# Two-layer encoder on one core: first transfers, step rates, and layer 0's attention and short convolution

## Chip, cores and metric

One core of a Trainium2 chip runs the whole kernel in one launch. The metric is the device time of a launch in microseconds (us). PE is TensorE (the matrix engine), DVE is VectorE, ACT is ScalarE, POOL is GpSimd, and SP is SyncE, whose queue issues all DMA transfers of this kernel.

## The reference

The input is x (256 positions, 2048 channels), a condition c (2048 values) and fp32 weights for two layers; everything is computed and returned in fp32. Cut to what matters:

```
c_act = silu(c)
for l in range(2):
    shift_m, scale_m, gate_m, shift_f, scale_f, gate_f = (c_act @ w_mod[l] + b_mod[l]) in 6 parts
    h = layer_norm(x) * (1 + scale_m) + shift_m
    uv, q_c, kv_c, k_r, sb, sc, sh, ag = split(h @ w_in[l])       # 4288 columns
    y_a = gelu(u) * spatial gating of layer_norm(gelu(v))
    y_b = latent attention: q = rms_norm(q_c) @ w_uq, k and v = rms_norm(kv_c) @ w_ukv,
          rotary parts on q and on k_r, softmax over a block-causal mask, 4 heads
    y_c = sb * conv3(sc * sh)                                     # short causal convolution
    y_d = silu(layer_norm(conv31(a * sigmoid(g))))                # a, g from ag
    x = layer_norm(ALPHA * x + (1 + gate_m) * (concat(y_a, y_b, y_c, y_d) @ w_out[l]))
    h = layer_norm(x) * (1 + scale_f) + shift_f
    x = layer_norm(ALPHA * x + (1 + gate_f) * ((silu(conv3(gate)) * val) @ w_down[l]))   # gate, val = h @ w_up[l]
```

## The kernel before

The 2048 channels are 16 tiles of 128 (KT = 16), the positions two tiles of 128. Weights stream from memory in units of 1 MB or less and are used once.

**Two ways to multiply.** A plain ("exact") unit loads fp32 weights into a buffer named `wexact` and PE multiplies them as fp32; the trace has two matmul instructions for each such product. A split unit loads into `wraw` (one of four raw buffers of 1 MB, shared with `wmod`), ACT rounds it to a high half `whi` (L390), DVE subtracts to get the low half `wlo` (L391), and PE does three products in place of one exact product: high by high, low by high, high by low. The activations are split the same way by ACT and DVE (`a`, L409 and L410). Layer 0's input projection and the last two column chunks of its output projection are exact, as are the first `PLAIN_UNITS` units of the first chunk; nearly all the rest is split.

**Modulation steps.** `w_mod` is read in 192 blocks of 1 MB. A block is one DVE instruction over 128x2048: a product with the condition's rows `crep` summed into a column (L194), or, for a gate, an accumulation of rows into `macc` (L205). Layer 0's first 32 blocks feed its first norm. The other 160 are doled out by a generator, `mods`: each unit that is loaded calls `pump`, which adds the phase's rate from `RATES` to a credit and takes one step for each whole credit. `need` takes what is missing at the place where a result is wanted. `STEPS` says how many background steps (the taps of the 31-wide convolution, L870 on ACT and L873 on DVE) run with a unit.

**Order.** Each engine runs its instructions in one fixed order. The tile framework makes that order when the kernel is built: by the program's order, with instructions that its own timing holds for ready let ahead. A `NoSync` dependency fixes the order of two instructions on one engine.

**Start.** The transfers are issued as: identity (`cst`), parameters (`par`), condition row (`crow`), the two halves of x, then `w_mod` and `w_in` blocks in turn. PE spreads `crow` over 128 rows (`ps_c`), ACT makes `crep` of it. DVE takes the statistics of x (L1466), POOL the power, and then DVE the first two `wmod` blocks, which wait for the power. ACT scales x (`xn`), PE transposes it (L1489), ACT modulates it (`hF`, L118), and the first products `D_c` run. After the transposes of the two halves, `warm` puts 8 and 14 products of the identity with itself on PE (`spare`, L1475; two instructions each).

**Layer 0's attention.** When the latents' sums are there (`B_w`, `B_n`), `mix_b` takes `MODS_AHEAD` gate steps, then ACT copies the latents to `lat`. In `attend`, PE turns them through two PSUM buffers that alternate (`ps_q`, `ps_q`, `ps_kv`, `ps_kr`, `ps_qn` and so on): ACT scales the queries' part `qg`, DVE forms the key's products `kc` (L1079, L1080) and the latents `kvr` (L1084), both kept behind the steps taken ahead, and PE then forms `ps_kr` and the queries `ps_qn`. The softmax takes maximum, reciprocal, scaling (L1177) and the copies of the turned probabilities (L1191 to L1195) on DVE, the exponential on ACT. The rest of layer 0's input projection (`C_c`) runs between these pieces. The short convolution `conv_c` has one ACT scaling and two DVE accumulations for each of 4 channel tiles (L1250, L1252).

**Output projection.** `out_proj` goes through three column chunks (1024, 512 and 512 wide); in the first, a unit is two channel tiles, 8 units in all. DVE adds the gate and the residual (`yg`, L632 on), and the norm follows.

Of the kernel before, what the change touches and what calls it, by code (L numbers as in the profile page):

```python
# [13 lines left out]
P = 128  # L14
# [18 lines left out]


RATES = [
    dict(B=1.3, attend=1.3, C=1.9, out=1.0, out_next=1.55, out_last=0.0, up=0.7, down=0.7, down_next=0.7, down_last=0.0),
    dict(D=1.0, U=0.0, V=0.0, B=0.0, C=0.0, E=0.9, attend=0.0, out=0.6, out_next=0.6, out_last=0.0, up=0.3, down=0.7, down_next=0.7, down_last=0.0),
]

STEPS = [  # L40
# [46 lines left out]
def encoder_kernel(ctx: ExitStack, tc: tile.TileContext, A: dict, consts: bass.AP, out: bass.AP):  # L87
    nc = tc.nc
    pe, act, dve, pool = nc.tensor, nc.scalar, nc.vector, nc.gpsimd

    keep = ctx.enter_context(tc.tile_pool(name="keep", bufs=1))
    rawp = ctx.enter_context(tc.tile_pool(name="rawp", bufs=4))
    splitp = ctx.enter_context(tc.tile_pool(name="splitp", bufs=4))
# [50 lines left out]
    def power(o, i):  # L144
        return pool.tensor_tensor(out=o, in0=i, in1=mhalf[:, : i.shape[1]], op=ALU.pow)

    X = []
    for t in range(2):
        x_t = keep.tile([P, D], F32, name=f"x{t}")
        X.append(x_t)  # L150

    par = keep.tile([P, -(-PARAMS // 16) * 16], F32, name="par")
    nc.sync.dma_start(out=par[:, 0:112], in_=A["params"][:, 0:112])
    crow = raw_tile("crow")
    nc.sync.dma_start(out=crow[0:1, :], in_=A["c"])
    for t in range(2):
        nc.sync.dma_start(out=X[t], in_=A["x"][0, t * P : (t + 1) * P, :])
    cact = keep.tile([P, 16], F32, name="cact")
    act.activation(out=cact, in_=par[:, 0:16], func=AF.Silu)

    crep = keep.tile([P, D], F32, name="crep")
    for i in range(4):
# [12 lines left out]
    plus_one(0, SCALE_M)  # L175
# [6 lines left out]


    MOD = {}
    last_step = [None]
    data_dep = mybir.DependencyInfo(mybir.DependencyClass.Sync, mybir.DependencyReason.DATA)
    order_dep = mybir.DependencyInfo(mybir.DependencyClass.NoSync, mybir.DependencyReason.DATA)

    def mod_block(l, m, kt, col):

# [9 lines left out]
    def mod_step(acc, w, kt, first):  # L200
        col = cact[:, kt : kt + 1]
        if first:
            i = dve.tensor_scalar(out=acc, in0=w, scalar1=col, scalar2=None, op0=ALU.mult)
        else:
            i = dve.scalar_tensor_tensor(out=acc, in0=w, scalar=col, in1=acc, op0=ALU.mult, op1=ALU.add)  # L205
        held(i, "mod")
        last_step[0] = i.ins.name

    def gate_rows(l, m, acc):

# [579 lines left out]
    def mixers(l, w_in, Y, hF=None, first_mod=None, quarter=None):  # L790
# [265 lines left out]
        def attend(WQ, WKV, lat, q01, rr):  # L1056
# [20 lines left out]
            by = turn(ps, S, [lat[t][:, 256:320] for t in range(2)])  # L1077
            kc = tmp_tile("kc")
            behind(dve.tensor_tensor(out=kc[0:64, 0:S], in0=by[0:64, :], in1=cosT[0:64, :], op=ALU.mult))  # L1079
            dve.tensor_tensor(out=kc[0:64, S : 2 * S], in0=by[0:64, :], in1=sinT[0:64, :], op=ALU.mult)  # L1080
            ps = ms_tile("ps_kv")
            for j in range(2):
                by = turn(ps, j * S, [lat[t][:, j * P : (j + 1) * P] for t in range(2)])
                behind(dve.tensor_scalar(out=kvr[:, j, :], in0=by, scalar1=KVG(j), scalar2=None, op0=ALU.mult))  # L1084

            rope = slot("rope").rearrange("p (j s) -> p j s", j=4)
            ps = ms_tile("ps_kr")
# [55 lines left out]
            def softmax(blk, g):  # L1143
                nkey = P * (blk + 1)
                per = 512 // nkey
                ps = ms_tile("ps_sc")
                for i in range(per):
                    h = g * per + i
                    o = ps[:, i * nkey : (i + 1) * nkey]
                    qs = slice(blk * P, (blk + 1) * P)  # L1150
                    mm(o, qn[:, h, qs], kn[:, h, :nkey], True, False)
                    mm(o, rope[:, h // 2, qs], rope[:, 2 + h % 2, :nkey], False, True)
                sm = smallp.tile([P, 16], F32, tag="sm", name="sm", bufs=3)
                p3 = ps.rearrange("p (i k) -> p i k", i=per)
                dve.memset(p3[0:64, :, nkey - 64 :], NEG)
                dve.tensor_reduce(out=sm[:, 0:per], in_=p3, axis=AX.X, op=ALU.max)
                dve.tensor_scalar(
                    out=sm[:, 4 : 4 + per],
                    in0=sm[:, 0:per],
                    scalar1=rr[:, 4 + blk : 5 + blk],  # L1160
                    scalar2=-1.0,
                    op0=ALU.mult,
                    op1=ALU.mult,
                )
                pt = tmp_tile("p")
                for i in range(per):
                    act.activation(
                        out=pt[:, i * nkey : (i + 1) * nkey],
                        in_=ps[:, i * nkey : (i + 1) * nkey],
                        func=AF.Exp,  # L1170
                        scale=rr[:, 4 + blk : 5 + blk],
                        bias=sm[:, 4 + i : 5 + i],
                        accum_out=sm[:, 8 + i : 9 + i],
                    )
                dve.reciprocal(out=sm[:, 12 : 12 + per], in_=sm[:, 8 : 8 + per])
                for i in range(per):
                    dve.tensor_scalar(  # L1177
                        out=pt[:, i * nkey : (i + 1) * nkey],
                        in0=pt[:, i * nkey : (i + 1) * nkey],
                        scalar1=sm[:, 12 + i : 13 + i],  # L1180
                        scalar2=None,
                        op0=ALU.mult,
                    )
                return pt

            def turned(pt, blk, g):
                ps = ms_tile("ps_pT")
                for i in range(4):
                    pe.transpose(ps[:, i * P : (i + 1) * P], pt[:, i * P : (i + 1) * P], ident)
                if blk == 0:  # L1190
                    dve.tensor_copy(pT0[:, :, 0:P], ps.rearrange("p (h s) -> p h s", h=4))  # L1191
                else:
                    p4 = ps.rearrange("p (h k s) -> p h k s", h=2, k=2)
                    dve.tensor_copy(pT0[:, 2 * g : 2 * g + 2, P : 2 * P], p4[:, :, 0, :])
                    dve.tensor_copy(pT1[:, 2 * g : 2 * g + 2, :], p4[:, :, 1, :])  # L1195

            p0 = softmax(0, 0)
            p1 = softmax(1, 0)
# [47 lines left out]

        def conv_c(ch):
            yc = Y["c"] = slot("yc").rearrange("p (j s) -> p j s", j=4)
            for j in range(4):
                act.activation(out=yc[:, j, :], in_=ch[:, j, :], func=AF.Copy, scale=SW(2, j))  # L1250
                for k in range(2):
                    dve.scalar_tensor_tensor(  # L1252
                        out=yc[:, j, 2 - k :],
                        in0=ch[:, j, : S - 2 + k],
                        scalar=SW(k, j),
                        in1=yc[:, j, 2 - k :],
                        op0=ALU.mult,
                        op1=ALU.add,
                    )
# [200 lines left out]
    def normed_T(hF):  # L1460

        mvs, rs = [], []
        for t in range(2):
            st = new_stats(f"in{t}")
            for c in range(4):
                dve.bn_stats(out=st[:, c, :], in_=X[t][:, c * 512 : (c + 1) * 512])  # L1466
# [214 lines left out]
```

## Time and profile before

| | us |
|---|---|
| median of 3 runs | 2220.2 |
| lowest and highest | 2219.65 and 2222.85 |
| the profiled execution's own time | 2218.97 |
| span of its instructions | 2217.2 |

| engine | busy us | share |
|---|---|---|
| PE | 2192.2 | 99% |
| DVE | 1715.6 | 77% |
| ACT | 1092.8 | 49% |
| POOL | 20.9 | 1% |

The shares are averages over stages with different limits. Matmuls are pipelined and their ends are modelled, so a busy PE can still be a PE that runs slower; start-to-start distances say more. "Idle before" a row is time in which the engine did nothing ahead of that instruction, with what ended it. PEclk is the share of full TensorE clock that was granted.

### The profile page before, as it was taken

How to read it: one execution, taken by the hardware profiler on the slowest of the kernel's cores; microseconds unless marked ns; L12 is line 12 of the kernel's file. 1: busy time of each engine (PE TensorE's matmuls, PEld its weight loads, DVE VectorE, ACT ScalarE, POOL GpSimd, SP SyncE). 2: the span in 40 equal slices, each digit the busy share in tenths (PEclk: the TensorE clock that was granted, in tenths of full speed). 3: DMA queues.
4: the chain of work that ended last, by engine and by line, in shares of the span. 5: the costliest groups of instructions: out<-in, count | busy, mean ns of one | idle time of the engine just before them, and what ended most of it. 6: DMA issues, size and time to landing. Idle time of an engine off the chain costs nothing. (4 is left out here: it accounts for less than half of the span.)

```text
span 2217.2 us, 28374 instructions
## 1 busy us (share of the span) xinstructions
PE 2192.2 (99%) x10880; PEld 1800.0 (81%) x10880; DVE 1715.6 (77%) x2197; ACT 1092.8 (49%) x1677; POOL 20.9 (1%) x38
## 2 busy tenths in 40 slices
PE   8999999999999999999999999999999999999997
PEld 6776875588888888888867988868888888888886
DVE  5657996799898889989958988867766656565776
ACT  3132740655554545545656555465455545454453
POOL 0000000000000000000000000000000000000000
PEclk9999999999999999999999999999999999999999
DMA  9999889688988888888757547846765555555553
GB/s 392 417 376 390 334 330 393 222 326 317 332 318 321 323 332 313 315 332 323 283 205 300 184 155 270 319 181 256 266 210 188 180 200 190 190 190 190 191 194 147
DMA packets 94033, 603.95 MB, mean 272 GB/s; under 512 B 10565, under 2 KB 10693, under 8 KB 29125
## 3 DMA queue, kind: packets, MB, share of 16 engines
q1 hardware_dynamic: 93898, 602.15, 73.2%
q8 instruction: 85, 1.39, 0.3%
q14 instruction: 50, 0.41, 0.1%
HBM read 600.01 MB, written 2.10 MB: 272 GB/s over the span
## 5 line engine op out<-in xcount | busy, mean ns | idle before, releaser
L390 ACT CAST whi<-wraw 128x1024 fp32r<-128x1024 f32 (+1 forms) x608 | 634.5, 1046 | 672.7 <-PE g_c L115 204.0
L391 DVE TENSOR_TENSOR wlo<-wraw,whi 128x1024 fp32r<-128x1024 f32 (+1 forms) x608 | 730.6, 1213 | 285.9 <-ACT whi L390 279.4
L115 PE MATMUL v_c<-hT,whi 128*128 128x512 f32 x1408 | 489.6, 391 | 0.0
L115 PE MATMUL g_c<-hT,whi 128*128 128x512 f32 x1280 | 444.7, 391 | 0.0
L115 PE MATMUL v_c<-hT,wlo 128*128 128x256 f32 x1408 | 394.4, 280 | 0.0
L115 PE MATMUL d<-whi,a 128*128 128x512 f32 x1344 | 386.2, 389 | 0.0
L115 PE MATMUL g_c<-hT,wlo 128*128 128x256 f32 x1280 | 358.4, 280 | 0.0
L194 DVE SCALAR_TENSOR_TENSOR wmod<-wmod,crep 128x2048 f32<-128x2048 f32 x128 | 292.2, 2286 | 39.9 <-DMA wmod<-in_w_mod_dram 39.2
L115 PEld LDWEIGHTS v_c<-hT,whi 128*128 128x128 f32 x1408 | 263.3, 187 | 57.6
L115 PEld LDWEIGHTS d<-whi,a 128*128 128x128 f32 x1344 | 252.1, 188 | 52.3
L115 PEld LDWEIGHTS g_c<-hT,whi 128*128 128x128 f32 x1280 | 239.4, 187 | 52.5
L115 PEld LDWEIGHTS v_c<-hT,wlo 128*128 128x128 f32 x1408 | 266.1, 189 | 0.2
L115 PEld LDWEIGHTS g_c<-hT,wlo 128*128 128x128 f32 x1280 | 241.9, 189 | 0.1
L115 PE MATMUL d<-wlo,a 128*128 128x512 f32 x672 | 232.9, 389 | 0.0
L205 DVE SCALAR_TENSOR_TENSOR macc<-wmod,cact,macc 128x2048 f32<-128x2048 f32 x60 | 140.8, 2347 | 17.0 <-DMA wmod<-in_w_mod_dram 16.5
L115 PEld LDWEIGHTS d<-wlo,a 128*128 128x128 f32 x672 | 126.1, 188 | 26.3
L115 PE MATMUL o<-whi,a 128*128 128x512 f32 x320 | 90.5, 390 | 0.0
L410 DVE TENSOR_TENSOR a<-g,a 128x512 fp32r<-128x512 f32 x132 | 88.7, 684 | 0.0
L534 PE MATMUL first<-wexact,hN 128*128 128x512 f32 x192 | 85.5, 596 | 1.2 <-ACT hN L118 0.8
L409 ACT CAST a<-g 128x512 fp32r<-128x512 f32 x132 | 81.1, 615 | 7.8 <-PE d L115 4.8
L1442 DVE SCALAR_TENSOR_TENSOR u<-g,par,u 128x254 f32<-128x254 f32 (+1 forms) x176 | 74.3, 478 | 0.4 <-ACT u L118 0.2
L115 PEld LDWEIGHTS o<-whi,a 128*128 128x128 f32 x320 | 59.8, 188 | 12.8 <-ACT whi L390 0.4
(317 smaller groups left out, 2375.7 us busy)
## 6 DMA issues: line engine op xcount, KB each, us to landing
wmod<-in_w_mod_dram SPq DMA_DIRECT2D x192, 1024.0 KB, 7.0
wraw<-in_ffn_w_up_dram SPq DMA_DIRECT2D x168, 1024.0 KB, 5.0
wraw<-in_ffn_w_down_dram SPq DMA_DIRECT2D x88, 1024.0 KB, 4.8
wexact<-in_w_in_dram SPq DMA_DIRECT2D x64, 512.0 KB, 10.0
wraw<-in_w_in_dram SPq DMA_DIRECT2D x24, 1024.0 KB, 5.1
wraw<-in_w_out_dram SPq DMA_DIRECT2D x22, 1024.0 KB, 5.8
wexact<-in_w_out_dram SPq DMA_DIRECT2D x20, 512.0 KB, 12.1
wexact<-in_ffn_w_up_dram SPq DMA_DIRECT2D x16, 512.0 KB, 6.3
```

Of the source, the lines that this page charges most:

```text
L115: pe.matmul(o, lhsT, rhs, start=start, stop=stop, skip_group_check=True)
L194: i = dve.scalar_tensor_tensor(out=raw, in0=raw, scalar=1.0, in1=crep, op0=ALU.mult, op1=ALU.mult, accum_out=col)
L205: i = dve.scalar_tensor_tensor(out=acc, in0=w, scalar=col, in1=acc, op0=ALU.mult, op1=ALU.add)
L390: held(act.copy(hi[:, :m], r), "cast")
L391: i = dve.tensor_tensor(out=lo[:, :m], in0=r, in1=hi[:, :m].bitcast(F32), op=ALU.subtract)
L409: act.copy(hi, src)
L410: dve.tensor_tensor(out=lo, in0=src, in1=hi.bitcast(F32), op=ALU.subtract)
L534: i = pe.matmul(ps, hN[kt // 4][:, kt % 4, t * P : (t + 1) * P], parts[kt], start=kt == 0, stop=kt == KT - 1, skip_group_check=True,)
L1442: dve.scalar_tensor_tensor(out=u[:, sh:], in0=x[:, : S - sh], scalar=col(k, j), in1=u[:, sh:], op0=ALU.mult, op1=ALU.add)
```

## The change

The condition row and x are transferred first, then the identity and the parameters. The first ACT function is called on a constant; `cact` is formed after `crep`, and the scale's "plus one" (DVE) after the statistics of x. The warm products are 6 and 6 in place of 8 and 14. Two orders are fixed on ACT behind `crep`. Rates: layer 0's up projection 0.7 to 0.6 steps a unit, layer 1's output projection 0.6 to 0.8. One plain unit in place of two in the first chunk of layer 0's output projection. In layer 0's attention two steps are taken ahead of the latents in place of three; the third comes after the key's products. Still in layer 0 alone, `kvr`, the softmax's scalings, the copies of the turned probabilities and all of the short convolution's scalings go to ACT; DVE adds the short convolution's taps in two wide instructions in place of eight.

```
-    dict(B=1.3, ..., up=0.7, down=0.7, ...),
-    dict(D=1.0, ..., out=0.6, out_next=0.6, ...),
+    dict(B=1.3, ..., up=0.6, down=0.7, ...),
+    dict(D=1.0, ..., out=0.8, out_next=0.8, ...),
...
-PLAIN_UNITS = 2
-MODS_AHEAD = 3
+PLAIN_UNITS = 1
+MODS_AHEAD = 2
...
+    X = [keep.tile([P, D], F32, name=f"x{t}") for t in range(2)]
+    crow = raw_tile("crow")
+    nc.sync.dma_start(out=crow[0:1, :], in_=A["c"])
+    nc.sync.dma_start(out=X[0], in_=A["x"][0, 0:P, :])
+    nc.sync.dma_start(out=X[1], in_=A["x"][0, P:S, :])
     cst = keep.tile([P, 1024], F32, name="cst")
     nc.sync.dma_start(out=cst[:, 0:128], in_=consts[:, 0:128])
...
-    act.activation(out=cact, in_=par[:, 0:16], func=AF.Silu)
+    act.activation(out=cact[:, 0:1], in_=ones[:, 0:1], func=AF.Silu)
...
-        act.activation(out=crep[:, i * 512 : (i + 1) * 512], in_=ps, func=AF.Silu)
+        creps.append(act.activation(out=crep[:, i * 512 : (i + 1) * 512], in_=ps, func=AF.Silu))
+    i = act.activation(out=cact, in_=par[:, 0:16], func=AF.Silu)
+    tc.add_manual_dep(i.ins, creps[3].ins.name, order_dep, ...)
...
-            dve.tensor_tensor(out=kc[0:64, S : 2 * S], in0=by[0:64, :], in1=sinT[0:64, :], op=ALU.mult)
+            i = dve.tensor_tensor(out=kc[0:64, S : 2 * S], in0=by[0:64, :], in1=sinT[0:64, :], op=ALU.mult)
+            if hF is not None:
+                next(mods, None)
+                tc.add_manual_dep(last_made[0].ins, i.ins.name, order_dep, ...)
...
-                behind(dve.tensor_scalar(out=kvr[:, j, :], in0=by, scalar1=KVG(j), scalar2=None, op0=ALU.mult))
+                if hF is not None:
+                    act.activation(out=kvr[:, j, :], in_=by, func=AF.Copy, scale=KVG(j))
+                else:
+                    dve.tensor_scalar(out=kvr[:, j, :], in0=by, scalar1=KVG(j), scalar2=None, op0=ALU.mult)
...
+                    p, r = pt[:, i * nkey : (i + 1) * nkey], sm[:, 12 + i : 13 + i]
+                    if hF is not None:
+                        act.activation(out=p, in_=p, func=AF.Copy, scale=r)
+                    else:
+                        dve.tensor_scalar(out=p, in0=p, scalar1=r, scalar2=None, op0=ALU.mult)
...
+                copy = dve.tensor_copy if hF is None else act.copy
...
         def conv_c(ch):
             yc = Y["c"] = slot("yc").rearrange("p (j s) -> p j s", j=4)
+            if hF is not None:
+                for j in range(4):
+                    act.activation(out=yc[:, j, :], in_=ch[:, j, :], func=AF.Copy, scale=SW(2, j))
+                for k in (1, 0):
+                    n = S - 2 + k
+                    t = actp.tile([P, 1024], F32, tag="act", name="scaledC").rearrange("p (j s) -> p j s", j=4)
+                    for j in range(4):
+                        act.activation(out=t[:, j, :n], in_=ch[:, j, :n], func=AF.Copy, scale=SW(k, j))
+                    dve.tensor_tensor(out=yc[:, :, 2 - k :], in0=yc[:, :, 2 - k :], in1=t[:, :, :n], op=ALU.add)
+                return
...
+        plus_one(0, SCALE_M)
...
-                    act.activation(out=r[:, 1:2], in_=mv[:, 0:1], func=AF.Copy, scale=-1.0)
+                    i = act.activation(out=r[:, 1:2], in_=mv[:, 0:1], func=AF.Copy, scale=-1.0)
+                    tc.add_manual_dep(i.ins, creps[2 + t].ins.name, order_dep, ...)
...
-                    warm(i, (8, 14)[t])
+                    warm(i, 6)
```

More of the change, by code (lines that the diff above doesn't have):

```diff
@@ L35 @@
 RATES = [
-    dict(B=1.3, attend=1.3, C=1.9, out=1.0, out_next=1.55, out_last=0.0, up=0.7, down=0.7, down_next=0.7, down_last=0.0),
-    dict(D=1.0, U=0.0, V=0.0, B=0.0, C=0.0, E=0.9, attend=0.0, out=0.6, out_next=0.6, out_last=0.0, up=0.3, down=0.7, down_next=0.7, down_last=0.0),
+    dict(B=1.3, attend=1.3, C=1.9, out=1.0, out_next=1.55, out_last=0.0, up=0.6, down=0.7, down_next=0.7, down_last=0.0),
+    dict(D=1.0, U=0.0, V=0.0, B=0.0, C=0.0, E=0.9, attend=0.0, out=0.8, out_next=0.8, out_last=0.0, up=0.3, down=0.7, down_next=0.7, down_last=0.0),
 ]
@@ L89, in encoder_kernel @@
     pe, act, dve, pool = nc.tensor, nc.scalar, nc.vector, nc.gpsimd
+    data_dep = mybir.DependencyInfo(mybir.DependencyClass.Sync, mybir.DependencyReason.DATA)
+    order_dep = mybir.DependencyInfo(mybir.DependencyClass.NoSync, mybir.DependencyReason.DATA)
     keep = ctx.enter_context(tc.tile_pool(name="keep", bufs=1))
@@ L145, in power @@
         return pool.tensor_tensor(out=o, in0=i, in1=mhalf[:, : i.shape[1]], op=ALU.pow)
[L147 to L150, printed above, removed]
     par = keep.tile([P, -(-PARAMS // 16) * 16], F32, name="par")
     nc.sync.dma_start(out=par[:, 0:112], in_=A["params"][:, 0:112])
[L154 to L157, printed above, removed]
     cact = keep.tile([P, 16], F32, name="cact")
-    act.activation(out=cact, in_=par[:, 0:16], func=AF.Silu)
+    act.activation(out=cact[:, 0:1], in_=ones[:, 0:1], func=AF.Silu)
     crep = keep.tile([P, D], F32, name="crep")
+    creps = []
     for i in range(4):
@@ L164, in encoder_kernel @@
         mm(ps, ones[0:1, :], crow[0:1, i * 512 : (i + 1) * 512], True, True)
-        act.activation(out=crep[:, i * 512 : (i + 1) * 512], in_=ps, func=AF.Silu)
+        creps.append(act.activation(out=crep[:, i * 512 : (i + 1) * 512], in_=ps, func=AF.Silu))
+    i = act.activation(out=cact, in_=par[:, 0:16], func=AF.Silu)
+    tc.add_manual_dep(i.ins, creps[3].ins.name, order_dep, reason="the condition's rows are there first")
     at = [16 + l * 425 for l in range(DEPTH)]
@@ L173, in plus_one @@
             dve.tensor_scalar(out=b, in0=b, scalar1=1.0, scalar2=None, op0=ALU.add)
-    plus_one(0, SCALE_M)
     def rest_of_constants():
@@ L184, in encoder_kernel @@
     MOD = {}
[L185 to L187 removed]
+    last_step, last_made = [None], [None]
     def mod_block(l, m, kt, col):
@@ L206, in mod_step @@
         held(i, "mod")
-        last_step[0] = i.ins.name
+        last_step[0], last_made[0] = i.ins.name, i
     def gate_rows(l, m, acc):
@@ L1079, in attend @@
             behind(dve.tensor_tensor(out=kc[0:64, 0:S], in0=by[0:64, :], in1=cosT[0:64, :], op=ALU.mult))
-            dve.tensor_tensor(out=kc[0:64, S : 2 * S], in0=by[0:64, :], in1=sinT[0:64, :], op=ALU.mult)
+            i = dve.tensor_tensor(out=kc[0:64, S : 2 * S], in0=by[0:64, :], in1=sinT[0:64, :], op=ALU.mult)
+            if hF is not None:
+                next(mods, None)
+                tc.add_manual_dep(last_made[0].ins, i.ins.name, order_dep, reason="the key's products come first")
             ps = ms_tile("ps_kv")
@@ L1480, in quarter @@
                 if q == 0:
-                    act.activation(out=r[:, 1:2], in_=mv[:, 0:1], func=AF.Copy, scale=-1.0)
+                    i = act.activation(out=r[:, 1:2], in_=mv[:, 0:1], func=AF.Copy, scale=-1.0)
+                    tc.add_manual_dep(i.ins, creps[2 + t].ins.name, order_dep, reason="the condition's rows are there first")
                     act.activation(out=r[:, 1:2], in_=r[:, 1:2], func=AF.Copy, scale=r[:, 0:1])
```

13 lines of the change are left out of this document (3 added, 10 removed).

## The prediction

> **What bounds the kernel.** I read the page first, then PE's waits, then the timeline of the stages that the change touches, and last the busy time by stage.
>
> ```profile
> span 2217.2 us, 28374 instructions
> PE 2192.2 (99%) x10880; PEld 1800.0 (81%) x10880; DVE 1715.6 (77%) x2197; ACT 1092.8 (49%) x1677; POOL 20.9 (1%) x38
> PE ps_c L115 <- DMA crow<-in_c_dram: 3.8, 1, 3.8
> ...
> PE ps_kr L115 <- DVE kc L1080: 1.0, 1, 1.0
> PE ps_q L1067 <- ACT lat L1037: 1.0, 1, 1.0
> ...
> PE ps_qn L115 <- DVE kvr L1084: 0.5, 1, 0.5
> PE V L115 <- DMA wexact<-in_w_in_dram: 0.4, 1, 0.4
> ```
>
> PE is the bound at 99%. So the change can gain only where PE stands, runs below its clock, or does products it need not do: the start, layer 0's attention, and the plain unit. Everything moved off DVE is worth nothing by itself. The profiled execution took 2218.97 us, 1.8 more than its span and 1.2 less than the median of 2220.2; I work against it and carry the difference over.
>
> **The start.**
>
> ```profile
> 1.18 0.42 SPq L153 DMA_DIRECT2D par<-in_params_dram  x1
> 2.02 0.82 SPq L157 DMA_DIRECT2D x<-in_x_dram  x2
> 7.01 2.47 DVE L1466 BATCH_NORM_STATS2 st_in<-x 128x6 f32<-128x512 f32 x4 [3.76 <-DMA x<-in_x_dram]
> 13.51 2.29 DVE L194 SCALAR_TENSOR_TENSOR wmod<-wmod,crep 128x2048 f32<-128x2048 f32 x1 [0.67 <-POOL rs_in L145]
> 16.76 3.29 PE L1475 MATMUL spare<-cst 128*128 128x128 f32 x28
> 18.31 0.60 ACT L118 ACTIVATE hF<-hF,mod 128x256 f32<-128x256 f32 x1 [0.77 <-DVE mod L1512]
> 19.88 1.03 PE L115 MATMUL D_c<-hF,wexact 128*128 128x256 f32 x4
> 45.50 1.98 PE L115 MATMUL V<-wexact,hF 128*128 128x512 f32 x4 [0.42 <-DMA wexact<-in_w_in_dram]
> 0.00:2.50 2.50, 0.00 (x0) 0.00 (x0) 0.00 (x0) 1.28 (x1) 0.51 (x8) 1.00 0.16 42
> 2.50:5.00 2.50, 1.19 (x2) 0.70 (x3) 0.25 (x2) 0.21 (x1) 0.00 (x0) 1.00 0.88 246
> 42.50:45.00 2.50, 2.50 (x12) 1.92 (x11) 0.80 (x1) 0.00 (x0) 0.00 (x0) 1.00 1.05 433
> ```
>
> The last three rows are stretches of 2.5 us; their last numbers are PEclk, DMA share and GB/s. From x's landing at 7.01 a DVE chain leads to `D_c`. x is issued two places earlier, at 1.18 in place of 2.02: 0.84 us. `hF` is ready at 18.91, but PE is in the 28 warm products until 19.88; with 12, at 3.29 / 28 = 0.12 each, they end 1.9 earlier, so PE could start 0.84 + 0.97 = 1.8 sooner. It can't keep that. At 45.50 it waits for weights, and the transfers run full (433 GB/s) all the way there. Only the nearly empty first stretch (42 GB/s) can be used better, and the identity and the parameters, 120 KB together, now stand between x and the weights (120 KB at 433 GB/s is 0.3 us). So 0.84 - 0.3 = 0.55, which I round to 0.6; the bounds are 0 (the stream no earlier) and 0.84 (all of it). `plus_one` goes into the 0.67 us in which DVE waits for POOL: nothing, 0.25 at most if that cover goes. [...]
>
> **Layer 0's attention.**
>
> ```profile
> 202.64 7.07 PE L115 MATMUL C_c<-hF,wexact 128*128 128x256 f32 x32
> 211.39 0.44 PE L1067 MATMUL ps_kv<-cst,lat 128*128 128x128 f32 x2 [0.23 <-ACT qg L1073]
> 212.87 0.67 PE L115 MATMUL ps_kr<-kc,cst 64*128 64x256 f32 x2 [1.04 <-DVE kc L1080]
> 215.83 7.67 PE L115 MATMUL ps_qn<-qg,wq 128*128 128x256 f32 x24 [0.54 <-DVE kvr L1084]
> 204.75 7.32 DVE L205 SCALAR_TENSOR_TENSOR macc<-wmod,cact,macc 128x2048 f32<-128x2048 f32 x3 [7.98 <-DMA wmod<-in_w_mod_dram]
> 211.99 0.41 DVE L1079 TENSOR_TENSOR kc<-ps_q,cst 64x256 f32<-64x256 f32 x1
> 215.30 0.47 DVE L1084 TENSOR_SCALAR kvr<-ps_kv,par 128x256 f32<-128x256 f32 x1
> 204.00:232.00 28.00, 25.84 (x106) 20.34 (x105) 23.63 (x23) 16.87 (x42) 1.50 (x3) 0.88 0.86 355
> 232.00:295.00 63.00, 63.00 (x293) 52.06 (x292) 62.03 (x76) 36.62 (x91) 0.00 (x0) 1.00 0.88 331
> 295.00:347.00 52.00, 51.85 (x206) 37.03 (x205) 49.79 (x66) 20.27 (x27) 0.70 (x1) 1.00 0.91 350
> ```
>
> DVE starts the three steps only when a block lands at 204.75 and is free at 212, when `kc` has been waiting since about 211.2. With two steps it is free at 209.6, so `kc` and `ps_kr` come 0.8 earlier, the latter at 212.05. The second `kvr` stands on DVE behind another 2.3 us step until 215.30, and `ps_qn` needs the buffer that it reads. On ACT, free there, it follows its transposes at once; `ps_kr` and the second `ps_kv` are then over by about 213.3, against 215.83: 2.5 us. The third step now queues behind `kc`; behind it stand only the convolution's taps, for which DVE stands idle later in this stretch (23.63 of 28 busy).
>
> Then the clock. 24 `ps_qn` take 7.5 us; at the rate of `C_c` (32 in 6.9) they would take 5.2. PEclk 0.88 over 28 us is 3.4 us of lost clock. It fell after some 2 us of PE idle between 209.9 and 213.5; the 1.0 us wait for `lat` just before left `C_c` at full rate. The change leaves about 1.2, nearer the second: I take the clock as kept, 2.3 us more. Together 4.8, with bounds of 0.8 (only `kc` moves) and 5.3. [...]
>
> **The softmax, the short convolution and the plain unit.**
>
> ```profile
> 297.06 13.90 PE L115 MATMUL o<-wexact,ya 128*128 128x512 f32 x32
> 1966.38 239.41 PE d L115 x1056
> L391 DVE TENSOR_TENSOR wlo<-wraw,whi 128x1024 fp32r<-128x1024 f32 x12 | 14.1, 1219 | 0.6 <-ACT whi L390 0.6
> L410 DVE TENSOR_TENSOR a<-yc,a 128x512 fp32r<-128x512 f32 x2 | 1.3, 679 | 0.0
> L1252 DVE SCALAR_TENSOR_TENSOR yc<-chC,par,yc 128x254 f32<-128x254 f32 (+1 forms) x8 | 3.4, 478 | 0.0
> L1177 DVE TENSOR_SCALAR p<-p,sm 128x128 f32<-128x128 f32 (+1 forms) x8 | 2.1, 306 | 0.0
> L1191 DVE COPY pT<-ps_pT 128x512 f32<-128x512 f32 x1 | 0.7, 684 | 0.0
> L1194 DVE COPY pT<-ps_pT 128x256 f32<-128x256 f32 x2 | 0.8, 418 | 0.0
> 277.37 1.61 ACT L870 ACTIVATE scaled<-gluD,par 128x226 f32<-128x226 f32 x4 [2.82 <-DVE convD L873]
> ```
>
> Two plain units are 32 instructions in 13.7 us from start to start, 6.85 a unit. A split unit is 2 x 2 x 2 x 3 = 24 products at 239.41 / 1056 = 0.227: 5.44. PE saves 1.4. DVE pays two `wlo` and one `a`, 2 x 1.22 + 0.68 = 3.1 us, in the stage where it is busy 49.79 of 52 us. It is freed of two `kvr` (0.9), the scalings (2.1), the copies (0.7 + 0.8, and as much for L1195, of the same form: 2.3) and eight accumulations (3.4) less two wide ones, priced as `wlo` (2.4): 6.3. The net is 3.2 us off a DVE that is nearly full from 232 to 347. ACT takes it on with 26 and 32 us of idle time in these two stretches, and was waiting for DVE (2.82 us) before a tap.
>
> So can DVE follow a PE that comes 0.6 + 4.8 + 1.4 = 6.8 us earlier? It gains 0.6 from the start, 3.2 here, and up to 4.4 of idle time in the attention (28 - 23.63), which ends when the latents come sooner: 3.8 to 8.2, with 6.0 in the middle. I take half of the plain unit's 1.4 as kept: 0.7. Bounds: -3.1 (DVE's new work falls on the path) and 1.4.
>
> **The rates.**
>
> ```profile
> 1376.00:1416.00 40.00, 40.00 (x180) 33.13 (x179) 32.03 (x31) 20.98 (x26) 0.00 (x0) 1.00 0.77 287
> 1416.00:1449.00 33.00, 33.00 (x147) 27.32 (x146) 32.72 (x38) 17.19 (x23) 0.00 (x0) 1.00 0.87 337
> 1453.29 0.69 DVE L632 TENSOR_TENSOR yg<-o,gate 128x512 f32<-128x512 f32 x1 [4.08 <-PE o L115]
> ```
>
> Layer 0's up projection calls `pump` 88 times, so it takes 52 steps in place of 61; PE does not wait there, and it gains nothing. The steps come later. Layer 1's output projection takes 10 in place of 7 (6 and 4 for 5 and 2). The one more in its first chunk goes into 8 us of idle time. The two more in the second, 2 x 2.29 = 4.6, fall where DVE is busy 32.72 of 33 us, with 4.08 behind: 0.5 is left over, and the last chunk's low halves come later. I take a loss of 0.6, between 0 and 4.6. Counted through both layers, the last step that the norm after it needs (the 144th) is taken when 145 are due: one to spare.
>
> **The sum.** 0.6 + 4.8 + 0.7 - 0.6 = 5.5 us. The profiled execution would take 2213.5, the median 2220.2 - 5.5 = 2214.7.
>
> **Rivals.**
> 1. The clock falls all the same. For it: PE's work between 209.9 and 213.3 stays thin. The gain is 5.5 - 2.3 = 3.2: 2217.0. Chance 0.10.
> 2. DVE becomes the bound up to 347, as its shares of 98% and 96% suggest: only its own 3.8 less the rates' 0.6 stay, and another 0.7 for stalls at the first split units: 2.5, so 2217.7. Against it: the idle time in the attention. Chance 0.10.
> 3. ACT's order, on the other side. A softmax scaling on ACT waits for a reciprocal on DVE that stands behind a 2.29 us step, and the convolution's four scalings (1.61 us) wait behind it, so DVE, the full engine, runs dry: 3.9 us for each of three softmax groups, 11.7 in all, 2220.2 - 5.5 + 11.7 = 2226.4. It makes the kernel slower by over 0.2% from 9.9 us of DVE idle time on. Against it: ACT was a whole tap ahead. Chance 0.12.
> 4. The attention's order does not change, since the framework puts the third step or the transposes elsewhere: 0.6 + 0.7 - 0.6, 2219.5. Chance 0.02.
>
> **The numbers.** The forecast has 0.66. Its own range is 2211.5 to 2217: at the low end all the good bounds hold (0.84 + 5.3 + 1.4 = 7.5, 2212.7) and the wait for `lat` (1.0) goes too. About 0.2% (4.4 us: below 2215.8 or above 2224.6) is what a measurement of this kernel can tell from no change. Of the forecast's 0.66, 0.04 lie within it, so faster is 0.62; the same is 0.04 + 0.10 + 0.10 + 0.02 = 0.26; slower 0.12. The range takes in the forecast and rivals 1, 2 and 4, 2211.5 to 2219.5, and leaves out rival 3 and some 0.05.
>
> **What would show it.** Right: `D_c` starts at about 18.1 and PE then waits longer for weights near 41 to 46; `ps_qn` starts some 3 us earlier, behind `ps_kr` and not behind a `kvr` on DVE, and its 24 take 5.2 us; PEclk near 1.00 there; the last `o` of the first chunk ends 5 to 7 us sooner, and the distance holds up to layer 1's output projection. Wrong: 24 `ps_qn` in 7 us or more (rival 1), PE waiting for `wlo` or `a` between 300 and 345 for over 2 us (rival 2), DVE waiting for `scaled` between 240 and 290 (rival 3), or PE waiting for `wlo` or `tlo` near 1445 for more than the 0.6.

## Result, and the profile after

| | before | after |
|---|---|---|
| median, us (6 runs each) | 2220.62 | 2228.62 |
| lowest and highest | 2218.76, 2222.85 | 2224.51, 2232.95 |
| profiled execution, its span | 2218.97, 2217.2 | 2230.01, 2228.2 |

The ratio is 1.0032, with a 95% interval of 1.0023 to 1.0042: slower by 0.3%, where 2214.7 was forecast. The page of the changed kernel, and its busy time by stage (the columns are PE, PEld, DVE, ACT, POOL, PEclk, DMA share, GB/s):

```profile
span 2228.2 us, 28372 instructions
PE 2198.2 (99%) x10868; PEld 1802.4 (81%) x10868; DVE 1713.5 (77%) x2179; ACT 1103.0 (50%) x1704; POOL 23.3 (1%) x38
204.00:232.00 28.00, 26.29 (x112) 20.76 (x111) 23.28 (x21) 20.68 (x51) 0.98 (x3) 0.94 0.76 311
232.00:295.00 63.00, 62.39 (x293) 52.13 (x291) 57.47 (x61) 38.91 (x101) 0.00 (x0) 1.00 0.96 365
295.00:347.00 52.00, 46.49 (x183) 35.08 (x184) 47.42 (x57) 24.48 (x35) 1.01 (x1) 0.93 0.78 289
```

DVE is less busy in the last two of these stages (57.47 and 47.42 us, against 62.03 and 49.79), and PE's share in the first two is much as before; the last stage, the output projection, stands out: PE is 5.5 us short of busy, and its clock is at 0.93 (before: 51.85 of 52 and 1.00). The timeline of PE at the places that the prediction named, first of the changed kernel:

```profile
18.02 0.70 PE L118 MATMUL D_c<-hF,wexact 128*128 128x256 f32 x2 [0.80 <-ACT hF L121]
41.33 3.26 PE L118 MATMUL D_c<-hF,wexact 128*128 128x256 f32 x14 [0.98 <-DMA wexact<-in_w_in_dram]
...
202.12 7.07 PE L118 MATMUL C_c<-hF,wexact 128*128 128x256 f32 x32
...
211.87 0.44 PE L1064 MATMUL ps_kv<-cst,lat 128*128 128x128 f32 x2 [0.56 <-ACT kvr L1085]
212.87 1.38 PE L118 MATMUL ps_kr<-kc,cst 64*128 64x256 f32 x4 [0.57 <-ACT kvr L1085]
214.18 6.83 PE L118 MATMUL ps_qn<-qg,wq 128*128 128x256 f32 x24
220.85 1.46 PE L118 MATMUL ps_qr<-qg,wq 128*128 128x256 f32 x6
...
292.50 1.89 PE L118 MATMUL ps_mean<-convD,ones 128*128 128x256 f32 x8
298.68 0.80 PE L118 MATMUL ps_var<-ones,sqD 128*128 128x1 f32 x4 [4.29 <-ACT sqD L904]
299.33 8.61 PE L118 MATMUL o<-wexact,ya 128*128 128x512 f32 x16
...
312.04 0.77 PE L118 MATMUL o<-wlo,a 128*128 128x512 f32 x2 [1.83 <-DVE wlo L388]
...
407.53 1.55 PE L531 MATMUL first<-wexact,hN 128*128 128x512 f32 x3
...
912.37 0.62 PE L118 MATMUL d<-whi,a 128*128 128x512 f32 x2
```

And the same places of the kernel before that are not in the prediction:

```profile
295.33 1.89 PE L115 MATMUL ps_mean<-convD,ones 128*128 128x256 f32 x8
...
310.79 1.84 PE L115 MATMUL ps_var<-ones,sqD 128*128 128x1 f32 x16
...
402.80 1.13 PE L534 MATMUL first<-wexact,hN 128*128 128x512 f32 x2
...
902.09 0.63 PE L115 MATMUL d<-whi,a 128*128 128x512 f32 x2
```

Subtracting the starts (after less before) shows where the time goes: -0.5 at `C_c` (202.12 and 202.64), -1.65 at `ps_qn`, -2.8 at `ps_mean`, then +2.3 at the first `o` (299.33 and 297.06), +4.7 at the next projection's first product, +10.3 at `d`, where layer 0's down projection begins, and +11 at the end. So the gain of 2.8 us was there at 292 us. Two losses ate it: 7.5 us between 292 and 350, and 5.5 us between 407 and 912; another 0.7 came behind them.

**The first loss** is read on ACT and DVE:

```profile
291.90 0.69 DVE L1227 TENSOR_TENSOR chC<-C_c,sc 128x512 f32<-128x512 f32 x1 [4.88 <-PE C_c L118]
...
303.62 1.29 DVE L1276 TENSOR_TENSOR yc<-yc,partE 128x512 f32<-128x512 f32 x2
...
292.69 1.71 ACT L1253 ACTIVATE yc<-chC,par 128x256 f32<-128x256 f32 x4 [2.86 <-DVE chC L1227]
294.31 3.28 ACT L1258 ACTIVATE scaledC<-chC,par 128x255 f32<-128x255 f32 x8
297.49 0.60 ACT L406 CAST a<-ya 128x512 fp32r<-128x512 f32 x1
298.00 0.63 ACT L904 ACTIVATE sqD<-convD 128x512 f32<-128x512 f32 x1
...
304.39 1.22 ACT L406 CAST a<-yc 128x512 fp32r<-128x512 f32 x2 [4.74 <-DVE yc L1276]
305.61 0.63 ACT L904 ACTIVATE sqD<-convD 128x512 f32<-128x512 f32 x1
306.14 3.87 ACT L387 CAST whi<-wraw 128x1024 fp32r<-128x1024 f32 x4
```

In the changed kernel the first `ps_var` products stand ahead of `o` on PE; the kernel before had them behind its two plain units, at 310.79. They need `sqD`, which on ACT stands behind the 12 short-conv scalings (292.69 to 297.5; eight of them, 3.28 us, are new on ACT) and a cast. PE waits 4.29 us at the head of its queue, while `ya` and its weights for `o` are there. Then unit 1, now split, needs `whi` and `wlo`: `whi` stands on ACT behind the cast of `yc`, which DVE delivers at 304.4, so PE waits another 1.83. That `yc` is no earlier than before is DVE's order: DVE stands 4.88 us ahead of `chC`, then runs from 292.77 to 309 without a gap, and has three modulation steps (2.2 us each) between `chC` and `yc`, where the kernel before had two. PEclk 0.93 over 52 us is 3.6 us of lost clock behind the two waits. Two waits and the clock make 4.3 + 1.8 + 3.6 = 9.7, and 1.4 comes back from the plain unit: 8.3 against the 7.5 seen, with the clock's two digits for the rest.

**The second loss** is no wait: PE issues fewer products in the same time at full granted clock (from 620 to 900 us 1586 against 1617 before, both with PEclk 1.00). Its cause is taken up with the last experiments.

### The profile page after: what moved, and what is told of

It is laid out like the page before. It is cut to its first block, busy times and chain, and to the rows that moved or that the text cites. A ratio compares the mean times of both kernels' runs of the same rounds, so it can differ in the third digit from the quotient of the medians.

```text
span 2228.2 us, 28372 instructions
## 1 busy us (share of the span) xinstructions
PE 2198.2 (99%) x10868; PEld 1802.4 (81%) x10868; DVE 1713.5 (77%) x2179; ACT 1103.0 (50%) x1704; POOL 23.3 (1%) x38
## 5 line engine op out<-in xcount | busy, mean ns | idle before, releaser
L118 PE MATMUL o<-whi,a 128*128 128x512 f32 x336 | 96.1, 394 | 0.0
```

Of the source, the lines that this page charges most:

```text
L118: pe.matmul(o, lhsT, rhs, start=start, stop=stop, skip_group_check=True)
```

## Experiments

### Each of the two waits taken away alone, and both together

The first kernel puts `ps_var` back behind the first unit of `o`; the second takes the short-conv's scalings back (as before, on ACT and DVE); the third has two plain units; the fourth is the second and third together.

```
 e_order:            + tc.add_manual_dep(i.ins, first_out[-1], order_dep, ...)   # i: a ps_var product,
                                                     # first_out[-1]: the last product of o's unit 0
 e_conv_dve:         - the branch 'if hF is not None:' of conv_c
 e_plain2:           PLAIN_UNITS = 1 -> 2
 e_plain2_conv_dve:  both of the last two
```

> The changed kernel with one order added on TensorE: the first ps_var product has to come behind the last product of the first unit of `o` (chunk 0), as it did in the kernel before. Nothing else differs. Theory T1 (the order is what costs): the 4.6 us in which TensorE stood for sqD ahead of the first `o` and the half clock of 3.41 us behind it (1.6 us) go, 6.2 us in all: about 2222.4 against 2228.6, a ratio to the kernel before of 1.001. Theory T2 (two walls in series: unit 1, now split, has its whi at 306.1 and its wlo at 310.8 whatever TensorE did before): the first `o` starts at about 294.5 but TensorE then stands 4 to 6 us at the first product of unit 1 that needs wlo, and the gain is 0 to 2 us, 2226.6 to 2228.6. In both, the pace of the up-projection's products in layer 0 (236 ns each in the changed kernel's profile, 230 in the kernel before's) is a matter of its own: if it is caused by the late output stage it is back at 230 here and 5.5 us go with it; if by the changed rates, it stays at 236.

> The changed kernel with the short-conv of layer 0's conv branch done as before (one product on ScalarE, two multiply-adds on VectorE for each of four tiles) in place of 12 scalings on ScalarE and two additions on VectorE. T1 (the scalings on ScalarE are what delays sqD, the cast of ya and whi of unit 1): ScalarE is free some 3 us earlier, the first `o` starts near 295, and 4 to 8 us go: 2220.6 to 2224.6, a ratio of 1.000 to 1.002. T3 (the amount of work on VectorE is the limit, as the prediction's second rival had it): VectorE gets about 1 us more to do ahead of the output stage, and the time is 2228.6 to 2230, a ratio of 1.004. T2 alone (unit 1's split is late whatever else is done): 2226 to 2229.

> The changed kernel with two plain output units again (unit 1 of the output projection goes with one weight term and no split, as before). T1 (the order costs 6.2 us ahead of unit 1): that stays, the 2.0 us wait for wlo at 312 and the half clock behind it (2.0 us) go, and the plain unit's saving of 1.4 us on TensorE is given up: about -2.6 us, 2226.0, a ratio of 1.0024. T2 (the split of unit 1 is the main loss): 4 to 8 us go, 2220.6 to 2224.6, a ratio of 1.000 to 1.002, with `o` starting near 299 all the same.

> Both of the last two edits: what is left of the change is the start, the attention's part (key products between the modulation steps, kvr, softmax scalings and ps_pT copies on ScalarE) and the rates. T1 and T2 together: the gain of 2.8 us that the changed kernel still had at ps_mean is kept through the output stage, so 2217.8 against 2220.6, a ratio of 0.9987, if the up-projection's products are back at 230 ns; 2223.3, a ratio of 1.0012, if the rates make them 236 ns. T3 (VectorE's amount of work is the limit): no gain is left at the first `o`, 2221 to 2223.

| kernel | median | ratio to before, 95% |
|---|---|---|
| order alone | 2225.84 | 1.0032 (1.0020 to 1.0044) |
| short-conv as before alone | 2228.07 | 1.0043 (1.0029 to 1.0058) |
| two plain units alone | 2227.02 | 1.0034 (1.0022 to 1.0046) |
| two plain units and short-conv as before | 2221.88 | 1.0005 (0.9996 to 1.0014) |

Undoing one gains nothing that these times show; undoing two gains the loss back. These kernels keep the changed rates, and their times also hold the second loss, which comes and goes (below). The start of the next projection's first product lies ahead of it and says the same: 407.53 in the changed kernel, 407.98, 409.37 and 409.07 with one undone, 403.07 with two, 402.80 before. PE's timeline, of the kernel with the order alone:

```profile
294.32 7.03 PE L122 MATMUL o<-wexact,ya 128*128 128x512 f32 x16
307.32 2.08 PE L122 MATMUL o<-whi,a 128*128 128x512 f32 x4 [5.96 <-ACT whi L393]
309.19 3.41 PE L122 MATMUL ps_var<-ones,sqD 128*128 128x1 f32 x16
```

of the kernel with the short-conv as before:

```profile
295.58 8.83 PE L122 MATMUL o<-wexact,ya 128*128 128x512 f32 x16 [1.89 <-DMA wexact<-in_w_out_dram]
306.81 1.77 PE L122 MATMUL o<-whi,a 128*128 128x512 f32 x4 [2.40 <-ACT whi L391]
309.76 1.22 PE L122 MATMUL o<-wlo,a 128*128 128x512 f32 x2 [1.18 <-DVE wlo L392]
```

and of the kernel with two plain units:

```profile
299.82 1.01 PE L122 MATMUL ps_var<-ones,sqD 128*128 128x1 f32 x4 [3.77 <-ACT sqD L908]
300.69 16.15 PE L122 MATMUL o<-wexact,ya 128*128 128x512 f32 x32
```

With the order alone `o` starts 5 us earlier and PE then stands 5.96 us at `whi`, which comes near 307 in any case. With plain units alone the wait of 3.8 us ahead of `o` stays. With the short-conv as before a new wait takes the place of the first, 1.89 us for the weights of `o`: they are issued at 289.71, against 285.26 in the changed kernel, so this edit is not the removal of one wait alone. So the two obstacles lie in series, as T2 had it for the first kernel (though PE waits at `whi` and not at `wlo`, and the median lies 0.8 us below T2's 2226.6). The second kernel took what T2 alone gave it. T1 reads the place right in the third, but its 6 us for the order alone and 4 to 8 us for the scalings alone fail, and so do T2's 4 to 8 us for the plain unit alone. T3 fails as a cause: between 232 and 410 us DVE is busy for 148.7 us in the fourth kernel and for 145.7 and 143.4 in the first and third, and the fourth is the fastest. But T3's time for it, 2221 to 2223, is the one that came, and not 2217.8: its `o` starts at 296.27, behind a wait of 1.76 us for the transfer of its weights. That is the next question.

Whether ACT's scalings are bad in themselves is asked by the other two edits together, with the short-conv left on ACT:

```
 e_order_plain2:  e_order, and PLAIN_UNITS = 1 -> 2
```

> The changed kernel with the first ps_var behind the first unit of `o` and with two plain units; the short-conv's scalings stay on ScalarE. Theory S (two obstacles in series, each of which hides the other): with both gone, the first `o` starts at 294.3 and unit 1 needs no split weights, so most of the 6.5 us come back: 2221 to 2223, a ratio of 1.0005, the rest being unit 2's split weights, whose load is issued at about 299 behind a step that stands behind chC on VectorE. If instead the short-conv on ScalarE is bad in itself (ScalarE late for the casts and whi whatever TensorE does first): TensorE stands 4 us or more at unit 2's wlo, and the time is 2224 to 2227, a ratio of 1.002 to 1.003.

2223.91, 1.0011 (1.0002 to 1.0021): between the two theories' times. `o` starts at 294.6 and runs both plain units through in 13.9 us, and the next projection starts at 403.85, 3.7 us earlier than in the changed kernel; so most of the loss goes with the scalings still on ACT. What remains is one wait at unit 2, shorter than the 4 us that the second theory gave:

```profile
294.60 13.90 PE L122 MATMUL o<-wexact,ya 128*128 128x512 f32 x32
...
313.36 1.04 PE L122 MATMUL o<-wlo,a 128*128 128x512 f32 x2 [2.61 <-DVE wlo L394]
```

### What the attention's part is worth

Two plain units, the short-conv and the rates as before: start and attention are all that is left of the change.

```
 PLAIN_UNITS = 1 -> 2;  conv_c as before;  up=0.6 -> 0.7;  out=0.8, out_next=0.8 -> 0.6, 0.6
```

> Of the change only the start and the attention's part are left (key products between the steps, kvr, softmax scalings and copies on ScalarE); two plain units, the short-conv on VectorE and the step rates are those of the kernel before. The kernel with the changed rates beside it took 2221.9, with its first `o` held 1.8 us by the transfer of its weights and its layer 1 some 1.5 us behind. If the rates cause the loss in layer 1: 2220.3, a ratio to before of 0.9999. If they do not: 2221.9 again, 1.0007. The prediction's sum for these parts (-5.4) would be 2215; it is expected to fail, since the weights of the first output unit are issued behind a modulation load at 290.5 us, and that load does not come earlier when the attention does.

2221.49, 1.0003 (0.9994 to 1.0012): not the 5.4 us of the sum, at best 1.3. It is 0.4 us from the same kernel with the changed rates (2221.88), so this pair shows no price of the rates. Yet `ps_mean` stands at 292.07, 3.3 us ahead of before. SP's queue, DVE and PE show where it goes (the rows of SP are issues of transfers):

```profile
279.98 9.90 SPq L194 DMA_DIRECT2D wmod<-in_w_mod_dram  x3
289.98 0.86 SPq L375 DMA_DIRECT2D wexact<-in_w_out_dram  x2
...
285.32 0.69 DVE L411 TENSOR_TENSOR a<-yb,a 128x512 fp32r<-128x512 f32 x1 [3.15 <-ACT a L410]
286.63 0.69 DVE L411 TENSOR_TENSOR a<-yb,a 128x512 fp32r<-128x512 f32 x1 [0.62 <-ACT a L410]
287.24 2.29 DVE L195 SCALAR_TENSOR_TENSOR wmod<-wmod,crep 128x2048 f32<-128x2048 f32 x1
...
295.74 14.00 PE L122 MATMUL o<-wexact,ya 128*128 128x512 f32 x32 [1.78 <-DMA wexact<-in_w_out_dram]
```

The weights of the first output unit are issued behind a `wmod` block. That block needs a raw buffer that a modulation step on DVE frees, and the step (287.24 to 289.5) stands behind two `a` instructions that wait for the attention's output. So the weights are issued at 289.98, and PE waits 1.8 us for them. The next kernel takes fewer steps ahead of these weights:

```
 e_step_later:  C=1.9, out=1.0, out_next=1.55  ->  C=1.75, out=1.0, out_next=1.55   (on the kernel above)
```

> As the kernel with start and attention alone, but with layer 0's rate in the stage C at 1.75 in place of 1.9, so that one modulation step fewer (and its 1 MB load) is queued ahead of the output projection's first weights; it is made up in a later stage. Theory L (what holds the first `o` is the queue of SyncE: its weights are issued behind a modulation load that waits for a step on VectorE): the issue moves from 290.5 to about 283, TensorE's wait of 1.8 us for the transfer goes, the gain of 2.7 us at ps_mean reaches the output stage, and the time is about 2 us under the kernel with start and attention alone: 2218.3, a ratio of 0.999. Theory V (VectorE's amount of work is what ends the stage): the step is only moved to a place where it delays yc or wlo by 2.2 us; no gain, 2220 to 2222.5.

```profile
279.77 2.54 SPq L194 DMA_DIRECT2D wmod<-in_w_mod_dram  x2
282.40 0.86 SPq L375 DMA_DIRECT2D wexact<-in_w_out_dram  x2
...
293.58 6.60 PE L122 MATMUL o<-wexact,ya 128*128 128x512 f32 x15
...
409.48 2.08 PE L535 MATMUL first<-wexact,hN 128*128 128x512 f32 x2 [9.26 <-ACT hN L125]
```

The mechanism is shown: the weights are issued at 282.40, PE does not wait for them, and `o` is 3.5 us ahead of before. The time was missed by far, 2233.06 and 1.0048 (1.0035 to 1.0062): the credit now reaches 46 steps where the norm at 400 us wants 48, not one fewer but two, and PE stands 9.26 us for them. The next three give the steps back in the last units (1.85 for 1.55): on the kernel with start and attention, on the one with the short-conv on ACT and `ps_var` in order, and, as a control, on the kernel before.

```
 C=1.9, out=1.0, out_next=1.55  ->  C=1.75, out=1.0, out_next=1.85
```

> The kernel with start and attention alone, with layer 0's rate in the stage C at 1.75 in place of 1.9 and in the last units of the output projection at 1.85 in place of 1.55: one modulation step is moved from ahead of the output projection's first weights to its last units, and all 48 steps that the norm at 400 us wants are taken (the kernel with 1.75 alone took 46 and stood 9.4 us there). Theory L (the queue of SyncE holds the first `o`): the gain of 3.5 us that that kernel showed at the first `o` and of 2.5 us at 400 us lasts to the end: about 1.5 to 2.5 us under the kernel with start and attention alone (2221.5), so 2219.0 to 2220.0, a ratio to before of 0.9990 to 0.9997. Theory V (the steps cost the same wherever they are): the wait comes back at 400 us as 1 to 3 us, and the ratio stays at 1.000.

> The changed kernel with ps_var behind the first unit of `o`, two plain units, and the same two rates (1.75 and 1.85). In the kernel without these rates TensorE stood 2.8 us at unit 2's wlo, whose load was issued behind a step that stood behind chC on VectorE. Theory L: the load is one step earlier, that wait goes wholly or for the greater part, and the time is 2 to 3 us under that kernel (2223.9): 2221 to 2222. Theory A (it is ScalarE's order, with 12 scalings ahead of the casts and of whi, that makes wlo late): the wait stays at 2 us or more and the time at 2223 to 2225.

> The kernel before with the two rates alone (1.75 and 1.85), as a control: there the first `o` waited for nothing that the queue of SyncE brings (it starts 1.73 us behind ps_mean, which is what ps_mean takes). Theory L: no gain without the earlier attention, 2220.0 to 2221.0, a ratio of 1.000. If the rates are a gain of their own: 2218 to 2219, and the same gain in the kernel with the attention is then not the attention's.

| kernel | median | ratio to before, 95% |
|---|---|---|
| start, attention, steps moved | 2221.20 | 0.9993 (0.9984 to 1.0002) |
| the same, short-conv on ACT, changed rates | 2224.22 | 1.0009 (1.0000 to 1.0018) |
| before, steps moved | 2224.67 | 1.0018 (1.0009 to 1.0026) |

The first is the lowest ratio of all, but its interval holds 1: no version here is shown to beat the kernel before. In its profile `o` starts without a wait, 1.3 us ahead of before. Some 1.6 us are lost in the clock: from 295 to 347 PE is almost without a gap (51.91 of 52 us busy), but PEclk is 0.97 (before: 51.85 and 1.00); the rest goes mainly in waits of 0.28 us at the last chunk's start and 0.40 at a `ps_xT`. The ratio is the one that theory L gave, the time is 1.2 us above it: the queue held the first `o`, as L had it, but the gain did not last. In the second, the wait for `wlo` fell from 2.6 to 0.4 us, as L said; the time did not follow, for the reason below. The control is slower than before by more than was expected: there PE waits 1.6 us at `ps_rD` for `dgD`, a place where its order changed too. So the attention's worth depends on where the steps stand: about nothing with them in place, 0.25% between the first and the third line with them moved, of which the control's own wait is a part.

### The pace of the up projection

> The changed kernel once more, as a second look at its layer 0 up projection. If the slower pace there (236 ns a product in place of 230 from 624 us on) belongs to the kernel, it is there again and the time is near 2230. If it comes and goes from one execution to the next, the pace is 230 in about half of the looks and the time is then near 2224.7, which is what the two fastest of its six runs took. The waits ahead of the first `o` (4.6 us) and at unit 1's wlo (2 us) are there in both cases.

The changed kernel once more took 2225.52. Busy time by stage, of the kernel before, of the changed kernel's profile and of this second one (the count behind PE's busy time is its products):

```profile
620.00:900.00 280.00, 280.00 (x1617) 246.87 (x1616) 245.72 (x286) 144.39 (x207) 0.00 (x0) 1.00 0.87 325
```

```profile
620.00:900.00 280.00, 280.00 (x1586) 242.64 (x1585) 229.91 (x288) 142.16 (x204) 0.00 (x0) 1.00 0.81 293
```

```profile
620.00:900.00 280.00, 280.00 (x1617) 247.11 (x1616) 234.82 (x294) 146.01 (x209) 0.00 (x0) 1.00 0.82 299
```

The same program issues 1586 or 1617 products in 280 us, 2% apart, both with PEclk 1.00 and nothing waiting. The second profile reaches `d` 4.8 us earlier than the first. From the projection's first product to `d` the kernel before and this profile take 499.3 us, the first profile of the changed kernel 504.8; one other profile shows the slow pace, that of the kernel with the steps moved and the short-conv on ACT (1587 products in these 280 us). In the first profile the pace changes at 624.2 us, 6 us behind the last of the `ps_gate` products of this projection (588 to 618 us here, 562 to 586 before): two products take 0.346 us up to there and 0.353 from there until the projection ends. The changed rate (0.6) is what puts the `ps_gate` products later, so the last two kernels go back to 0.7, on the changed kernel and on the second kernel of the last table:

```
 up=0.6 -> 0.7;  out=0.8, out_next=0.8 -> 0.6, 0.6
```

> The changed kernel with the step rates of the kernel before (0.7 in layer 0's up projection, 0.6 in layer 1's output projection), all else as changed. Theory R (the lower rate brings the slow pace: of eight profiles at 0.6 two have it, of five at 0.7 none, and the spread of times splits into two groups mostly at 0.6): the slow pace goes, the times stand in one group round 2224.7 to 2225.5, a ratio of 1.0018 to 1.0022. Theory N (the slow pace has nothing to do with the rates): two groups as in the changed kernel, some 5.5 us apart, and a median of 2225 to 2229, a ratio of 1.003.

> The kernel with ps_var behind the first unit, two plain units, the rates 1.75 and 1.85 and the short-conv's scalings on ScalarE, now with 0.7 and 0.6 for the two rates that the change touched. With the changed rates its times stood in two groups, 2219.7 to 2222.4 (4 of 11) and 2224.2 to 2226.5 (7 of 11). Theory R: the upper group goes, the median is 2219.5 to 2221, a ratio of 0.9993 or below. Theory N: both groups stay, the median 2222 to 2225.

The changed kernel with the old rates took 2225.64, 1.0024 (1.0015 to 1.0033), and its ten runs lie between 2224.89 and 2227.23, where the changed kernel's six spread over 8.4 us. The medians lie 3.0 us apart, taken at different times, and the two intervals overlap; the one narrow group is what speaks for theory R, though its median lies 0.1 us above R's times and within N's. Nor is a narrow group the rule at 0.7: start and attention alone spread over 5.2 us. The other took 2221.07, 1.0004 (0.9995 to 1.0014), with 5 of 12 runs above 2223, so the upper group did not go there as R had it; its profile, of a run of 2223.78, shows one reason:

```profile
440.00:560.00 120.00, 120.00 (x681) 104.06 (x680) 107.82 (x121) 61.86 (x89) 0.00 (x0) 1.00 0.88 322
620.00:900.00 280.00, 280.00 (x1617) 246.87 (x1616) 246.39 (x290) 145.06 (x207) 0.00 (x0) 1.00 0.88 321
```

Here the slow pace lies ahead of the gate products (681 products in 120 us, where the kernel before has 694) and is gone behind them (1617 in 280). All seven profiles at 0.7 have the fast pace behind the gate products (1616 to 1618), six of eight at 0.6. What sets the pace on entry stays open, and so does why the old rate always left it fast.

## Why the prediction was wrong

- **Start, 0.6:** right. 0.5 at `C_c`, `D_c` at 18.02, and the longer wait for weights at 41 (0.98), as told.
- **Attention, 4.8:** half of it, 2.3 (2.8 less the start's 0.5). `ps_qn` came 1.65 us earlier, not 3, because `ps_kv` and `ps_kr` each wait 0.56 for `kvr` on ACT. So the stretch of transposes kept 1.7 us of PE idle time (0.35, 0.23, 0.56 and 0.57) where the prediction counted on 1.2; the kernel before had 1.6 there, not some 2. The clock was not kept: the 24 `ps_qn` took 6.7 us (220.85 - 214.18), between rival 1's 7 and the forecast's 5.2. Nor do those four waits settle the clock: they are the same to 0.01 us in the changed kernel, in start and attention alone and in the same with the steps moved, but PEclk from 204 to 232 was 0.94, 1.00 and 0.88 there. In all 13 profiles with the new attention it was 1.00 in three, 0.94 in seven and 0.88 in three: none, 1.7 or 3.4 us of lost clock in 28 us. PE's rows of start and attention, without and with the steps moved:

```profile
214.08 5.45 PE L122 MATMUL ps_qn<-qg,wq 128*128 128x256 f32 x24
```

```profile
214.31 8.22 PE L122 MATMUL ps_qn<-qg,wq 128*128 128x256 f32 x24
```

  In the changed kernel PEclk was 0.50 from 213.6 to 217.0, in the kernel before from 213.5 to 220.35, and 1.00 on both sides; the changed kernel's two other stretches at 0.50 up to 347 us, 299.0 to 302.4 and 312.6 to 316.0, lasted 3.4 us too. What sets when such a stretch comes is not shown. A forecast of this term has to be a spread of some 2.8 us (5.3 to 8.1), not a value.
- **Short-conv, softmax and plain unit, 0.7 gained, bounds -3.1 to 1.4:** this is the step that failed; it lost 7.5. The working summed busy times by engine: DVE relieved by 3.2 us, ACT with 26 and 32 us idle. Neither engine had more to do than it could: DVE is less busy in both stages and stands 4.88 us ahead of `chC`, waiting for PE, and ACT is idle for 24 and 28 us. But ACT's idle time was not where the scalings went: they stand in one block ahead of the casts, `sqD` and `whi` of the output stage, and the framework let `ps_var` ahead of `o`. The prediction asked what each engine has to do, and not what stands behind the moved work on its new engine. Nor was the plain unit's price the sum of two `wlo` and one `a`: it made `whi` needed 6.85 us earlier, when DVE had not yet delivered the `yc` whose cast stands ahead of `whi` on ACT. DVE's 4.88 idle us could not serve there, since `chC` had to come first in its order; whether one of the three modulation steps taken in them would have brought `yc` forward was not tried. The bounds, made of busy times, could not hold a wait.
- **Rates, 0.6 lost, bounds 0 to 4.6:** wrong place. Layer 1's output projection shows no wait between 1440 and 1470. If the rates have a price, it lies in layer 0's up projection, which was taken to gain and lose nothing: 0 or 5.5 us by the pace, 3.0 between the medians with and without them (2228.62 and 2225.64), 3.1 between those of the second kernel of the last table and its own (2224.22 and 2221.07), but 0.4 with start and attention alone (2221.88 and 2221.49); not settled beyond that.
- **Rivals:** rival 1 came about for half. Rival 2's sign (`wlo` late by over 2 us) was just missed at 1.8. Its cause, the sum of DVE's work over the stages, is not borne out, since that sum fell; but DVE's gapless stretch from `chC` on does lie on the way to `whi` and `wlo`. Rival 3 had the side, a time not far off (2226.4) and the mechanism, work in ACT's order, but in another place: between 232 and 295 DVE waited only for `C_c`; the block that hurt was the short-conv's, and what waited was PE.
- **The range:** its low end, 2211.5, is 0.2 us below what its own terms give (2212.7 less 1.0).

## What to carry to other kernels

Work moved to an engine with idle time costs what stands behind it in that engine's order (here 4.29 us at `ps_var`), so for each moved block name the next instruction that the bounding engine waits for, and when it is needed. When undoing one suspect gains nothing, undo two: obstacles in series hide each other (2225.84 to 2228.07 us with one undone, 2221.88 with two). A load that is queued behind a buffer's release does not come earlier when its consumer does (issued at 289.98 us, though `ps_mean` came 3.3 us earlier); find the step that frees the buffer first.

## What was not expected of the hardware

A steady stream of two products in turn (512 and 256 columns wide), at PEclk 1.00, ran at two paces, 2% apart (1586 or 1617 in 280 us), in the same program; the slow one set in 6 us behind the last `ps_gate` product and then held to the end of the projection, with 228 or 229 products in each 40 us. The same stretch of layer 0's attention, with its waits the same to 0.01 us in three profiles, lost none, 1.7 or 3.4 us of clock in 28 us (PEclk 1.00, 0.94 or 0.88; 24 products in about 5.3, 6.7 or 8 us from start to start).
